# A hybrid diffusion layer: the opening by token halves in written order, matrix-memory pools reused tile by tile, S3 and S4 lows behind the first weight sums

## The chip, the cores and the metric

The kernel runs on one core of one Trainium2 chip, as one program for one launch. The metric is device time in microseconds, the median of several executions. Engines: PE (TensorE, matrix products), DVE (VectorE), ACT (ScalarE), POOL (GpSimd) and SP (SyncE, whose instruction queue issues most transfers).

## The reference

One layer of a diffusion trunk over 640 tokens (512 latent, 128 context), width 1024, feed-forward width 2816, all float32:

```python
def layer(x, mods, l, p, ctx):
    m = [mods[:, j][:, None, :] for j in range(N_MOD)]      # mods = silu(c) @ w_ada + b_ada, 9 x 1024
    g = p['g_norm'][l]
    hh = rmsnorm(x, g[0]) * (1 + m[1]) + m[0]
    x = x + 0.5 * m[2] * swiglu(hh, p['ffn1_w1'][l], p['ffn1_w3'][l], p['ffn1_w2'][l])
    hh = rmsnorm(x, g[1]) * (1 + m[4]) + m[3]
    y, ctx_out = token_mixer(hh, p, l, ctx)      # differential attention || bidirectional mLSTM
    x = x + m[5] * y
    hh = rmsnorm(x, g[2]) * (1 + m[7]) + m[6]
    x = x + 0.5 * m[8] * swiglu(hh, p['ffn2_w1'][l], p['ffn2_w3'][l], p['ffn2_w2'][l])
    return x, ctx_out

def swiglu(h, w1, w3, w2):
    return (jax.nn.silu(h @ w1) * (h @ w3)) @ w2
```

## The kernel before

**Products.** Features lie on partitions, tokens along the free axis, in two halves of 320 (`HALF`). A float32 product is made of three fast ones: each operand is split into a high part (`act(h, raw, Copy)` on ACT) and a low part (`raw - h` on DVE), and `mm3` sums high x high, high x low and low x high. Weights come in granules of 256 output columns, `raw` of 1 MB in a ring of two; of a granule that is used plainly, `wH` and `wL` are the parts.

**Feed-forward up, Strassen-like.** The up products (11 granule pairs of w1 and w3, blocks `b` 0 to 10) run as seven products instead of eight (`Granule`, `HalfStep.products`). Per granule they take weight sums: `parts` makes the small pieces `wB`, `wC` and changes `raw` in place; `sums` then makes the large pair `ww` from it (an ACT pass of 2048 columns and a DVE subtraction, whose instruction is `split_at`). On the token side they take the operands A11, A12, A22 (normed tokens) and S1, S2, S3, S4 (sums of them, high and low), which `operand_sums` makes once, each from two pieces `r`: eight sums `terms` and eight `low` on DVE, eight passes on ACT. Order per granule: A11, S1, S2, A12, S3; the last two, A22 and S4, run inside the next granule. Block 0 is always plain.

**The opening** (`Modulate`): x comes in two half loads; `Stats` makes the sum of squares of each half (ACT squares, DVE adds, `ps_ss` with a matrix of ones sums over partitions), `rstd` its reciprocal root (`rv`, Ln, Exp, and three refining operations of `newton_rsqrt`). For each of the eight feature tiles k, 1 MB of modulation weights is loaded (`raw_a`), `product(k)` (`ps_a`) gives a row, `columns(k)` (`ps_at`) turns it into columns `mod` and `scale`, and `norm` makes the normed tile of both halves, high and low. Block 0's products then run over k, three of its four units at once; the fourth follows. The lows of one of its two weight granules are made on POOL.

**Who sets the order.** A scheduler places instructions on each engine's queue by simulated readiness, within what data and buffers allow. `tc.keep_in_program_order` pins an instruction to the written order (all matmuls are pinned, and the transfers issued by `dma` while `in_order` is set); `tc.issue_after(ins)` holds instructions behind another. A pool with `reuse_waits="tile"` lets a new tile wait for the old tiles that it overlaps; a pool without waits for the whole old pool.

**From attention to matrix memory.** `Fill` is a queue of projection granules whose units are put between the steps of attention; `fill.drain()` runs it empty after the last head, `H.finish()` turns and stores the last head's output (`ps_aT`, `aT`), and `att.close()` gives up attention's pools. Then pools `mp` and `ps3` open, the mask, `csil2` (conditioning, 1 MB) and head 0's `va`, P and C are loaded, and two units of the gate projection `w_gd[1]` and five `prep` steps (`ps_k`, `ps_st`) precede the first cell (`ps_n`). `P` is a row of stabilisers broadcast over partitions, in two loads, plus a mask.

**The second feed-forward** works as the first. Its `operand_sums(…, True)` gives back an instruction (the second low of S2) behind which the next granule's `parts` are held, and a function that makes the lows of S4 later.

Of the kernel before, what the change touches and what calls it, by code (L numbers as in the profile page):

```python
# [31 lines left out]
def tile_trunk(ctx: ExitStack, tc: tile.TileContext, a: dict):  # L32
    nc = tc.nc
    act = nc.scalar.activation
    vec = nc.vector
    pool_e = nc.gpsimd

    def tt(eng, out, in0, in1, op):
        return eng.tensor_tensor(out=out, in0=in0, in1=in1, op=op)  # L39

    def stt(out, in0, scalar, in1, op0, op1):
        return vec.scalar_tensor_tensor(out=out, in0=in0, scalar=scalar, in1=in1, op0=op0, op1=op1)  # L42

    def ts(out, in0, s1, op0, s2=None, op1=None):
        if s2 is None:
            vec.tensor_scalar(out=out, in0=in0, scalar1=s1, scalar2=None, op0=op0)
        else:
            vec.tensor_scalar(out=out, in0=in0, scalar1=s1, scalar2=s2, op0=op0, op1=op1)
# [45 lines left out]
    for hf in range(2):  # L94
        dma(x_all[:, :, hf * HALF : (hf + 1) * HALF], a["x"][:, :, hf * HALF : (hf + 1) * HALF])
    sel = load(cp, [128, 2], a["sel"], name="sel")
    b_ada = load(cp, [128, 72], a["b_ada"], name="b_ada")
    g_norm = load(cp, [128, 3, KT], a["g_norm"], name="g_norm")
# [173 lines left out]
    class Whole(Granule):  # L272


        def split(self, fp=None):
            flat = self.raw.rearrange("p k n -> p (k n)")
            n = 512 * self.nk
            if fp is None:
# [5 lines left out]
            for (c0, c1, h), (_, _, lw) in zip(*t):  # L284
                act(h, flat[:, c0:c1], AF.Copy)
                tt(vec, lw, flat[:, c0:c1], h.bitcast(F32), ALU.subtract)
# [8 lines left out]
    class HalfStep:  # L295
# [29 lines left out]
        def gate_plain(self, f, hf, p):  # L325
            s = self.silu_tile(f, hf)
            act(s, p[0], AF.Silu)
            tt(vec, self.SO[:, self.Q[f, hf]], p[1], s, ALU.mult)

        def operand_sums(self, pair, hold=False):  # L330
# [30 lines left out]
            for f, i, r in (  # L361
                (terms, S1, 0), (terms, S1, 1), (terms, S3, 0), (low, S1, 0), (terms, S2, 0), (low, S1, 1), (terms, S3, 1),
                (terms, S2, 1), (low, S2, 0), (low, S2, 1), (low, S3, 0), (low, S3, 1), (terms, S4, 0), (terms, S4, 1),
            ):
                f(i, r)
                if (f, i) == (low, S2):
                    behind = prev.ins

            def last():
                low(S4, 0)  # L370
                low(S4, 1)

            if hold:
                return behind, last
            last()
            return behind

# [34 lines left out]
        def products(self, work, between, then=(), behind=None, prepared=False):  # L412
# [8 lines left out]
            if not prepared:  # L421
                work[0][0].parts(self.fp)
                work[0][0].sums()
            for i, (gr, A, done, used) in enumerate(work):
# [10 lines left out]
                if not last:  # L435
                    with tc.issue_after(behind if i == 0 and behind is not None else gr.split_at):
                        work[i + 1][0].parts(self.fp)
# [83 lines left out]
        def run_whole(self, x, gate, final, between):  # L521


            work = self.up_work()
# [10 lines left out]
            self.products(work, between, down[:2])  # L535
# [37 lines left out]
        def run(self, x, gate, final, behind=None, after=None):  # L573
# [23 lines left out]
            self.products(work, between, down[:2], behind=behind)  # L597
# [107 lines left out]
    with ExitStack() as ph:  # L705
# [11 lines left out]
        class Modulate:  # L717


            def __init__(self):  # L720
                self.raw, self.row = {}, {}
                self.rs = []
                x = [x_all[:, d, :] for d in range(KT)]
                st = [Stats(x, hf, ntmp) for hf in range(2)]
                for hf in range(2):
                    for d in range(KT):
                        st[hf].add(d)
                    self.rs.append(st[hf].rstd(psum))
                self.load(0)

            def weights(self, w1, w3):

                W = [[wp.tile([128, 2048], F32R, tag="w" + t, name="wH") for t in "HL"] for _ in range(2)]
                raws = [rawp.tile([128, 2048], F32, tag="raw", name="raw") for _ in range(2)]
                for k in range(2):
                    cs = slice(1024 * k, 1024 * k + 1024)
                    for raw, src, (h, lo), eng in zip(raws, (w1, w3), W, (pool_e, vec)):
                        dma(raw[:, cs], src[:, 4 * k : 4 * k + 4])
                        act(h[:, cs], raw[:, cs], AF.Copy)
                        tt(eng, lo[:, cs], raw[:, cs], h[:, cs].bitcast(F32), ALU.subtract)  # L740
                    self.load(k + 1)
                self.load(3)
                return W

            def load(self, k):
                self.raw[k] = load(fp, [128, 2048], a["w_ada_k"][k], tag=("s1", "s2", "s4", "SO")[k % 4], name="raw_a")

            def product(self, k):
# [9 lines left out]
                vec.tensor_copy(self.row[k], ps[:, :256])  # L758
                if k + 4 < KT:
                    self.load(k + 4)  # L760
                if k + 4 == KT - 1:
                    dma(ident, a["ident"])
                    in_order[0] = False

            def columns(self, k):
# [7 lines left out]
                for hf in range(2):  # L773
                    self.norm(hf, k)

            def norm(self, hf, d):

                c0 = hf * HALF
                S = hs.hh(d, hf)
                for s0, s1, j in SEGS[hf]:  # L780
                    xs = x_all[:, d, s0:s1]
                    h, lo = (t[:, s0 - c0 : s1 - c0] for t in S)
                    sh = m_of(0)[:, d, j : j + 1]
# [1240 lines left out]
```

## Time and profile before

| | |
|---|---|
| median of 3 runs | 1869.46 us (1865.64 to 1871.78) |
| profiled execution | 1868.63 us, span 1866.7 us |
| mean granted TensorE clock | 0.99 |
| loads of the first 60 us | 15.38 MB |
| DMA over the span | 299.81 MB, mean 161 GB/s |

How to read the rows. A timeline row has start, duration, engine, line, operation, out<-in, shapes, the number of merged instructions, and in brackets the idle time before it on its engine and what ended it. Line numbers are those of the kernel before; most operations are recorded in a helper (L52 `mm`, L39 `tt`, L42 `stt`, L74 `dma`). A row that begins with `A:B` is a stretch: length, then busy time and count on PE, PEld (weight loads), DVE, ACT and POOL, the mean granted clock, the DMA share and GB/s. Of the page, one row has busy times and shares, another the shares of the chain of waits that ended last.

### The profile page before, as it was taken

The numbers are of one execution on the slowest core, as the hardware profiler recorded it, in microseconds if no ns is written. First come the engines' busy times: TensorE is split into PE (matmuls) and PEld (weight loads), VectorE is DVE, ScalarE is ACT, GpSimd is POOL, SyncE is SP. The second block draws the span as 40 slices with busy tenths as digits, with TensorE's granted clock in tenths as the row PEclk, the third lists the DMA queues.
The fourth block names the chain that finished last, engine by engine and source line by source line (L and its number), as shares of the span: only waits on it lengthen the run. The fifth ranks groups of instructions, "written<-read, shape, count | busy, mean of one in ns | idle before, by whom it ended". The sixth has DMA issues, their size and how long they took to land.

```text
span 1866.7 us, 30740 instructions
## 1 busy us (share of the span) xinstructions
PE 1811.2 (97%) x12658; PEld 1773.0 (95%) x12658; DVE 1303.5 (70%) x2193; ACT 842.6 (45%) x1439; POOL 35.9 (2%) x57
## 2 busy tenths in 40 slices
PE   5899999999999999999999989999999999999999
PEld 4899999999998999999999989999999999999999
DVE  6888886577776675775755537885365878887585
ACT  5644444112454453553544436566234555554232
POOL 1000001110000000000000000000000000000000
PEclk8999999999999999999999999999999999999999
DMA  8344547964324323232222254556533344447872
GB/s 329 119 142 169 192 169 258 373 220 153 104 91 137 116 70 106 89 107 97 98 77 67 94 164 137 187 194 220 186 112 118 110 167 154 175 169 257 328 280 87
DMA packets 127293, 299.81 MB, mean 161 GB/s; under 512 B 9457, under 2 KB 90609, under 8 KB 114353
## 3 DMA queue, kind: packets, MB, share of 16 engines
q1 hardware_dynamic: 117890, 257.49, 39.9%
q0 software_dynamic: 9264, 40.37, 6.0%
q8 instruction: 99, 1.62, 0.4%
q14 instruction: 40, 0.33, 0.1%
HBM read 234.20 MB, written 63.63 MB: 160 GB/s over the span
## 4 chain that ended last, share of the span: by engine, by line
PE 86%; DVE 7%; DMA 4%; ACT 1%; issue 1%; SPq 0%; DVEq 0%; ACTq 0%
PE ps_f L52 40%; PE ps_p L52 22%; PE ps_t L52 12%; PE sc L52 2%; PE ps_o L52 2%; PE ps_n L52 2%; DMA ada<-csil_dram 2%; PE ps_u L52 1%; DVE ww L39 1%; PE ps_wT L55 1%; PE ps_qkT L55 1%; DMA raw<-in_w2b 1%; DMA P<-nm_dram 1%; DMA raw_a<-in_w_ada_c 0%; DVE junk L688 0%
## 5 line engine op out<-in xcount | busy, mean ns | idle before, releaser
L52 PE MATMUL ps_f<-S,ww 128*128 128x320 f32 x1992 | 322.0, 311 | 8.7 <-ACT ww L267 4.2
L52 PEld LDWEIGHTS ps_f<-S,ww 128*128 128x128 f32 x1992 | 300.1, 189 | 11.7 <-DVE ww L39 6.3
L52 PE MATMUL ps_p<-hH,wH 128*128 128x320 f32 x864 | 274.1, 317 | 3.6 <-ACT aT L1337 2.5
L52 PE MATMUL ps_p<-hH,wL 128*128 128x320 f32 x864 | 267.7, 310 | 0.0
L52 PE MATMUL ps_p<-hL,wH 128*128 128x320 f32 x864 | 267.6, 310 | 0.0
L52 PE MATMUL ps_f<-hm,ww 128*128 128x320 f32 x1248 | 198.8, 312 | 2.3 <-DVE ww L39 2.3
L52 PEld LDWEIGHTS ps_f<-hm,ww 128*128 128x128 f32 x1248 | 188.7, 190 | 2.8 <-DVE ww L39 2.6
L52 PE MATMUL ps_t<-wH,hH 128*128 128x256 f32 x640 | 186.4, 291 | 1.0 <-DVE x L42 1.0
L52 PE MATMUL ps_t<-wH,hL 128*128 128x256 f32 x640 | 182.6, 285 | 0.0
L52 PE MATMUL ps_t<-wL,hH 128*128 128x256 f32 x640 | 182.4, 285 | 0.0
L52 PEld LDWEIGHTS ps_p<-hH,wH 128*128 128x128 f32 x864 | 163.0, 189 | 5.0 <-ACT aT L1337 2.7
L39 DVE TENSOR_TENSOR ww<-raw,ww 128x2048 fp32r<-128x2048 f32 (+1 forms) x62 | 138.7, 2237 | 37.0 <-ACT ww L267 21.7
L52 PEld LDWEIGHTS ps_p<-hL,wH 128*128 128x128 f32 x864 | 163.0, 189 | 0.5
L52 PEld LDWEIGHTS ps_p<-hH,wL 128*128 128x128 f32 x864 | 162.8, 188 | 0.0
L52 PE MATMUL ps_f<-hm,wB 128*128 128x320 f32 x1008 | 161.5, 309 | 0.0
L52 PEld LDWEIGHTS ps_f<-hm,wB 128*128 128x128 f32 x1008 | 151.3, 188 | 0.0
L39 DVE TENSOR_TENSOR wL<-raw,wH 128x2048 fp32r<-128x2048 f32 x49 | 112.1, 2288 | 40.2 <-ACT wH L123 40.1
L123 ACT ACTIVATE wH<-raw 128x2048 fp32r<-128x2048 f32 x49 | 93.6, 1911 | 89.6 <-PE ps_p L52 85.1
L39 DVE TENSOR_TENSOR raw<-raw 128x1024 f32<-128x1024 f32 x144 | 124.6, 866 | 1.9
L52 PEld LDWEIGHTS ps_t<-wH,hH 128*128 128x128 f32 x640 | 123.8, 194 | 2.0 <-issue 1.2
L52 PEld LDWEIGHTS ps_t<-wH,hL 128*128 128x128 f32 x640 | 123.9, 194 | 0.5 <-DVE hL L42 0.5
L52 PEld LDWEIGHTS ps_t<-wL,hH 128*128 128x128 f32 x640 | 124.0, 194 | 0.2
(296 smaller groups left out, 3195.3 us busy)
## 6 DMA issues: line engine op xcount, KB each, us to landing
g_dram<-g SPq DMA_DIRECT2D x44, 640.0 KB, 4.3
raw_a<-in_w_ada_c SPq DMA_DIRECT2D x24, 512.0 KB, 4.0
raw<-in_w1b SPq DMA_DIRECT2D x11, 1024.0 KB, 4.8
raw<-in_w3b SPq DMA_DIRECT2D x11, 1024.0 KB, 4.9
raw<-in_w1a SPq DMA_DIRECT2D x10, 1024.0 KB, 4.8
raw<-in_w3a SPq DMA_DIRECT2D x10, 1024.0 KB, 6.1
ada<-in_w_ada_c POOLq DMA_DIRECT2D x18, 512.0 KB, 5.2
hm<-g_dram POOLq DMA_DIRECT2D x7, 1280.0 KB, 9.5
```

The source lines that it names most:

```text
L39: return eng.tensor_tensor(out=out, in0=in0, in1=in1, op=op)
L52: tc.keep_in_program_order(nc.tensor.matmul(*args, **kw))
L55: tc.keep_in_program_order(nc.tensor.transpose(*args, **kw))
L123: act(h, raw, AF.Copy)
```

## The change

**The opening** is rewritten (`Opening`) and by token halves. x comes in four quarters; the order of all loads is written out; the two weight granules of block 0 come in four pieces each, of 0.26 MB. Squares are made over two tiles at a time, half on ACT, half on DVE. Half 0's four units run over k first (`first`, with `step`), and modulation rows and columns, the division by the root, the norm of half 0, the splits of the weights, and half 1's statistics are put between its matmuls; half 1's four units run next (`second`). Between `as_written[0] = True` and `False`, ACT and DVE instructions are pinned to the written order too. POOL does nothing here. Block 1's w1 granule is taken plainly (`Whole`), its parts in tiles that are free at that time, and the Strassen-like granules start with block 1's w3.

**The operand sums.** `operand_sums` now makes S1 and S2, and the terms of S3, and gives back two functions: `third` (the lows of S3), which `products` runs behind the first granule's `split_at`, ahead of the next granule's `parts`; and `fourth` (terms and lows of S4), which both feed-forwards run behind the next granule's `split_at`. In the first feed-forward the column modulation (`csil`, `columns.place`) begins behind `fourth`.

**Matrix memory.** Pools `mp` and `ps3` reuse tile by tile; the granule `w_gd[1]` is queued before the last head ends and kept over `fill.drain(1)`; head 0 is loaded P first, then `va` and C, then `csil2`, in written order.

```diff
+    as_written = [False]
+    def placed(ins):
+        if as_written[0]:
+            tc.keep_in_program_order(ins)
+        return ins
...
-    for hf in range(2):
-        dma(x_all[:, :, hf * HALF : (hf + 1) * HALF], a["x"][:, :, hf * HALF : (hf + 1) * HALF])
+    def load_x(hf, r):
+        dma(x_all[:, 4 * r : 4 * r + 4, hf * HALF : (hf + 1) * HALF], a["x"][:, 4 * r : 4 * r + 4, hf * HALF : (hf + 1) * HALF])
+    for r in range(2):
+        load_x(0, r)
...
             for f, i, r in (
                 (terms, S1, 0), (terms, S1, 1), (terms, S3, 0), (low, S1, 0), (terms, S2, 0), (low, S1, 1), (terms, S3, 1),
-                (terms, S2, 1), (low, S2, 0), (low, S2, 1), (low, S3, 0), (low, S3, 1), (terms, S4, 0), (terms, S4, 1),
+                (terms, S2, 1), (low, S2, 0), (low, S2, 1),
             ):
...
+            return of((low, S3, 0), (low, S3, 1)), of((terms, S4, 0), (terms, S4, 1), (low, S4, 0), (low, S4, 1))
...
+            if ahead is not None:
+                with tc.issue_after(work[0][0].split_at):
+                    behind = ahead()
...
+        def step(ps, k, hf, between=None):
+            h, lo = hs.hh(k, hf)
+            for m, (w, v) in enumerate(((0, h), (1, h), (0, lo))):
+                for (f, i), p in ps.items():
+                    col = 256 * k + 128 * f
+                    mm(p, W[i][w][:, col : col + 128], v, start=k == 0 and m == 0, stop=k == KT - 1 and m == 2)
+                if m == 0 and between is not None:
+                    between()
...
+        load_weights(0)
+        start.load(1)
+        start.load(2)
+        load_x(1, 0)
+        load_weights(1)
+        start.load(3)
+        load_x(1, 1)
+        load_weights(2)
+        psum.order = [4, 5, 6]
+        for r in range(2):
+            start.squares(0, r)
+            start.add_squares(0, r)
+        start.product(0)
+        start.load(4)
+        load_weights(3)
+        start.rstd(0)
+        split_weights(0, "high")
+        start.refine(0)
+        start.columns(0)
+        start.divide(0, 0)
+        start.product(1)
+        split_weights(0, "low")
+        start.norm(0, 0)
+        start.load(5)
...
         for k in range(KT):
+            def ahead(k=k):
+                if k + 1 < KT:
+                    start.columns(k + 1)
+                if k == 5:
+                    start.refine(1)
+                if k >= 6:
+                    start.divide(1, k - 6)
+                if k % 2 and k < 6:
+                    split_weights((k + 1) // 2, "low")
+                elif k % 2 == 0 and k + 2 < KT:
+                    start.divide(0, (k + 2) // 2)
+                if k + 1 < KT:
+                    start.norm(0, k + 1)
+                if k % 2 == 0 and k < 6:
+                    split_weights(k // 2 + 1, "high")
+            step(first, k, 0, ahead)
+            if k + 2 < KT:
+                start.product(k + 2)
+                if k < 2:
+                    start.load(k + 6)
+            if k in (3, 4):
+                start.add_squares(1, k - 3)
+            if k in (1, 2):
+                start.squares(1, k - 1)
+            if k == 4:
+                start.rstd(1)
+            if k >= 6:
+                start.norm(1, k - 6)
...
+        for f, hf in ((0, 1), (1, 1), (0, 0), (1, 0)):
+            p = acc_tile(psum)
             for k in range(KT):
-                hs.plain(ps[i], W[i], 1, 1, k)
...
+                mm3(p, whole.w(0, k, f), whole.w(1, k, f), *hs.hh(k, hf), k == 0, k == KT - 1)
+            gate_first(f, hf, p, None)
+        with tc.issue_after(end.ins), tc.issue_after(at_act.ins):
+            third, fourth = hs.operand_sums(lambda r: x_all[:, 2 * r : 2 * r + 2, :])
...
+            fill.granule(a["w_gd"][1], lambda: feat_units(psum, gate_evac(mp, gd_dram, 1)))
             fill.one()
             fill.one()
-            fill.drain()
+            fill.drain(1)
             H.finish()
...
-    mp = ml.enter_context(tc.tile_pool(name="ml", bufs=1))
-    psum = ml.enter_context(tc.tile_pool(name="ps3", bufs=8, space=PSUM))
+    mp = ml.enter_context(tc.tile_pool(name="ml", bufs=1, reuse_waits="tile"))
+    psum = ml.enter_context(tc.tile_pool(name="ps3", bufs=8, space=PSUM, reuse_waits="tile"))
...
-    mem[0].load()
+    in_order[0] = True
+    mem[0].load(dma)
     mem[0].load_c()
+    csil2 = ada_p.tile([128, 2, D], F32, name="csil")
+    dma(csil2, csil_dram.partition_broadcast(128))
+    in_order[0] = False
+    columns.place(10, csil2, load_columns, 1)
...
-    summed, last_lows = hs.operand_sums(lambda r: x_pairs[r], True)
+    third, fourth = hs.operand_sums(lambda r: x_pairs[r])
```

More of the change, by code (lines that the diff above doesn't have):

```diff
@@ L410, in copy_of, with products @@
             return t
-        def products(self, work, between, then=(), behind=None, prepared=False):
+        def products(self, work, between, then=(), ahead=None, prepared=False):
             n = len(work)
@@ L571, in run_whole, with run @@
                     unit(G[-1], j, f, 1)
[L573 removed]
+        def run(self, x, gate, final, ahead, after):
             def nothing(*args):
@@ L715, in tile_trunk @@
         hs = HalfStep(1, fp, ntmp, psum, a["w1a"], a["w3a"], a["w2a"], FB)
-        class Modulate:
+        class Opening:
             def __init__(self):
[L721 to L743, printed above, removed]
@@ new lines, in tile_trunk @@
+        as_written[0] = True
+        start = Opening()
+        start.load(0)
+        for t, n in ((sel, "sel"), (b_ada, "b_ada"), (g_norm, "g_norm")):
+            dma(t, a[n])
+        load_weights(0)
[11 more added lines that the diff above has]
+        start.product(0)
@@ L842, in tile_trunk @@
+        with tc.issue_after(end.ins), tc.issue_after(at_act.ins):
+            hs.work[0][0].parts(fp)
+            hs.work[0][0].sums()
+        hs.store_g(hs.SO, 0)
         columns = Columns(56)
```

256 lines of the change are left out of this document (147 added, 109 removed).

## The prediction

> **What bounds the kernel now.** I read the page's busy shares and its chain of waits first.
>
> ```profile
> PE 1811.2 (97%) x12658; PEld 1773.0 (95%) x12658; DVE 1303.5 (70%) x2193; ACT 842.6 (45%) x1439; POOL 35.9 (2%) x57
> PE 86%; DVE 7%; DMA 4%; ACT 1%; issue 1%; SPq 0%; DVEq 0%; ACTq 0%
> ```
>
> TensorE is the bound, and 86% of the chain is its work. A change that keeps the matmuls can win only what TensorE loses elsewhere: before its first useful product, in waits, and at half clock after a wait. So I read the timeline for the idle times in its brackets, then the stretches around them for the granted clock (the number after the five engines). First the opening, with the rows of other engines that time its steps:
>
> ```profile
> 8.20 0.47 ACT L177 ACTIVATE nacc<-x 128x320 f32<-128x320 f32 x1 [4.22 <-DMA x<-in_x]
> 12.60 1.43 PE L52 MATMUL ps_ss<-nacc,ones 128*128 128x320 f32 x2 [12.60 <-DVE nacc L39]
> 15.13 0.49 DVE L48 TENSOR_SCALAR rv<-ps_ss 128x320 f32<-128x320 f32 x1
> 16.92 0.49 DVE L42 SCALAR_TENSOR_TENSOR rt<-ry 128x320 f32<-128x320 f32 x1 [0.30 <-ACT ry L160]
> 17.92 2.35 POOL L39 TENSOR_TENSOR wH<-raw,wH 128x1024 fp32r<-128x1024 f32 x1 [17.47 <-ACT wH L739]
> 17.97 2.65 DVE L42 SCALAR_TENSOR_TENSOR ry<-rt,ry 128x320 f32<-128x320 f32 x1
> 19.11 1.58 PE L52 MATMUL ps_a<-raw_a,small 128*32 128x256 f32 x16
> 22.07 0.41 DVE L758 COPY small<-ps_a 128x256 f32<-128x256 f32 x1
> 23.33 0.15 DVE L39 TENSOR_TENSOR mod<-ps_at,b_ada 128x4 f32<-128x4 f32 x1
> 27.60 1.01 PE L52 MATMUL ps_at<-sel,small 128*128 128x2 f32 x4 [3.06 <-DVE small L758]
> 30.41 4.45 PE L52 MATMUL ps_f<-hm,wH 128*128 128x320 f32 x18
> 34.70 0.50 PE L52 MATMUL ps_at<-sel,small 128*128 128x2 f32 x4
> 35.13 1.07 PE L52 MATMUL ps_a<-raw_a,small 128*32 128x256 f32 x16
> 55.98 12.56 PE L52 MATMUL ps_f<-hm,wH 128*128 128x320 f32 x84
> 68.38 1.92 PE L52 MATMUL ps_f<-hm,wB 128*128 128x320 f32 x12
> 84.07 0.56 PE L52 MATMUL ps_f<-S,ww 128*128 128x320 f32 x2 [4.22 <-ACT ww L267]
> 86.40 3.03 PE L52 MATMUL ps_f<-S,ww 128*128 128x320 f32 x10 [1.77 <-DVE ww L39]
> 92.19 1.92 PE L52 MATMUL ps_f<-S,ww 128*128 128x320 f32 x12
> 23.00:34.00 11.00, 7.94 (x52) 5.59 (x52) 9.48 (x21) 5.27 (x11) 2.57 (x1) 0.53 1.02 421
> 85.00:92.00 7.00, 5.60 (x21) 5.60 (x22) 5.60 (x6) 1.91 (x1) 0.00 (x0) 0.51 0.87 307
> ```
>
> The first useful product (`ps_f`) starts at 30.41, and the 11 us that end soon after it ran at a mean clock of 0.53. Block 0 is done at 68.38. Unhindered, a 320-column product takes (68.38 - 55.98) / 84 = 0.148 us. Between 68.38 and 92.19 TensorE did eight groups of twelve; less one group (1.77), the 84 products that a first granule needs were done at 90.42. That is 22.0 us for 12.4 us of work: two waits for the second granule's `ww`, 4.22 and 1.77, and half clock (0.51) behind them. VectorE made the sixteen operations of the S operands ahead of that `ww`.
>
> **Part 1, the opening.** *To the first product.* Work now goes by token halves, so the first product waits for the statistics of half 0 alone. All of half 0 was there at 8.20; in two pieces, the squares of the second piece start then. The 640-wide operations and the other sizes used below:
>
> ```profile
> 61.57 1.55 DVE L39 TENSOR_TENSOR x<-x 128x640 f32<-128x640 f32 x2
> 70.97 0.69 DVE L39 TENSOR_TENSOR wC<-raw,wC 128x512 fp32r<-128x512 f32 x1
> 84.05 2.29 DVE L39 TENSOR_TENSOR ww<-raw,ww 128x2048 fp32r<-128x2048 f32 x1 [1.98 <-ACT ww L267]
> ```
>
> Two VectorE operations of 0.78 bring it to 9.8. The first piece's pair of ones-products (two matmuls with the matrix of ones, 15.13 - 12.60 = 2.5 at this clock) runs beside them, the second pair ends at about 13.0. Then, written in this order: the first modulation product 1.58, its copy 0.41 (it stands ahead of `rv` on VectorE), from `rv` to the first refining step 1.8 as before (16.92 - 15.13), three such steps at 0.49, `mod` and `scale` at 0.15, the division of two tiles 0.78, half an ACT pass of 320 columns 0.47: 13.0 + 1.6 + 0.4 + 1.8 + 1.5 + 0.3 + 0.8 + 0.5 = 19.9, and 0.4 for hand-overs, **20.3 against 30.41, a gain of 10.1**. Part of it is the refining step that took 2.65 beside POOL's 2.35; the change has no POOL work there.
>
> *From there to the end of block 0* was 68.38 - 30.41 = 37.97. The 192 products stay. Past the new starting point lie one more modulation product (1.07), one more `ps_at` (0.50) and half 1's four ones-products (0.6 each at full clock, half of 2.5 / 2): +4.0. The clock: before, TensorE worked from 27.60 and the clock rose at about 34, so 3.5 us of half clock fell on products, a loss of 1.7; now all 6.4 us do, 3.2: +1.5. VectorE and ACT run in written order there. A step with modulation takes TensorE 12 x 0.148 + 1.07 + 0.50 = 3.3; VectorE has in step 1 two weight lows (1.38), two squares (1.56), `mod`/`scale`, a 320-wide low and a copy (1.2): 4.1; in step 5 three refining steps (1.5), two lows (1.4) and 1.2: again 4.1. So I allow +1.7 for these two; in the other steps VectorE has 2 to 3. Sum +7.2, **block 0 ends at about 65.5, 2.9 earlier**.
>
> *The first granule.* Its w1 is now multiplied plainly: 96 products, 14.2, instead of 84 in 22.0. They need no S operand and hide VectorE's work on those: ten operations at 0.78 for S1, S2 and their lows, the next weights' sums with their ACT pass, gating. S1 and `ww` are due at 65.5 + 14.2 + 1.8 = 81.5. VectorE's second-half work needs only what is loaded by then, so it can start on the S operands near 61: ten at 0.78, two gates and one store's low (2.5), parts of the weights (five operations, 4.5 from the 0.69 row and twice that for the double width), the wait for ACT's pass 2.0, `ww` 2.29, together 19.1: ready at 80. If that cover is gone it costs what the rival below says. The next granule's parts, the S3 lows (1.6) and its `ww` then come out within 0.5 of their due time: +0.5. Term: 14.2 + 0.5 - 22.0 = -7.3. **Opening: -10.2**; between -14 (no VectorE delay, earlier clock, no wait) and -2 (a start 3 later, both delays doubled, the rival's wait).
>
> On the clock, this trace has 6.4 us from steady work to full clock. The Trainium skill (TensorE: Matmul & The Clock Gate, Part 1) has the gate open after one busy window of about 3.4 us of a free-running counter. This trace took longer; by the page's figure the sum would be 1.5 us lower.
>
> The change moves the column modulation's 1 MB load, its ACT pass and its POOL loads behind the first granule's sums; its first user is a granule later, some 10 us away, so I cost it at nothing; without that cover, the brackets of 1.77 to 4.22 us above are the size of one such wait.
>
> **Part 2, from attention to matrix memory.**
>
> ```profile
> 1101.00 0.41 PE L52 MATMUL ps_p<-hH,wH 128*128 128x320 f32 x1 [2.47 <-ACT aT L1337]
> 1103.26 0.32 SPq L1553 DMA_DIRECT2D csil<-csil_dram  x1
> 1104.69 3.87 SPq L1579 DMA_DIRECT2D P<-nm_dram  x2
> 1114.18 0.83 DVE L39 TENSOR_TENSOR P<-P,mask 128x640 f32<-128x640 f32 x1 [10.55 <-DMA P<-nm_dram]
> 1117.46 1.20 PE L52 MATMUL ps_n<-va,P 128*128 128x258 f32 x2 [4.29 <-DVE P L39]
> 1102.00:1106.00 4.00, 4.00 (x19) 4.00 (x18) 0.27 (x5) 0.00 (x0) 0.00 (x0) 0.57 0.83 208
> 1116.00:1123.00 7.00, 5.54 (x14) 4.44 (x15) 4.56 (x12) 4.65 (x17) 0.00 (x0) 0.52 0.92 296
> ```
>
> Four losses: the first product waits 2.47 for the last ACT copy, because the new PSUM pool waits for the whole old one; half clock follows, 4 x 0.43 = 1.7; `ps_n` waits 4.29 for P; half clock again, (1123 - 1117.46) x 0.48 = 2.7. Together 11.2. With waits by tile the first product takes a bank whose evacuation is older: I take 2.2 and 1.6 of the first two. P is now the first load of SP's sequence there, ahead of `va`, C and the 1 MB of `csil`, which was ahead of it. Issued even as late as 1103.3, two issues of 1.9 and a transfer of about as much land it at about 1109; mask, ten ACT passes and the product with `ps_st` need some 3 more us, so `ps_n` can start where `ps_st` ends, 4.3 earlier. I take 3.6 and 2.0 of these two, leaving the rest to `va` and C. Who is queued behind P on SP are `va`, C, `csil`, and stores of `stage`; the column tile that reads `csil` comes several cells later. **-9.4**; between -11.2 and 0, 0 if both pools' tiles still wait for the last reader.
>
> **Part 3, the second feed-forward's S operands.**
>
> ```profile
> 1483.57 2.29 DVE L39 TENSOR_TENSOR ww<-raw,ww 128x2048 fp32r<-128x2048 f32 x1 [4.00 <-ACT ww L267]
> 1485.91 1.73 PE L52 MATMUL ps_f<-S,ww 128*128 128x320 f32 x10 [1.64 <-DVE ww L39]
> ```
>
> A loss of 1.64, no fall of the clock. Two S4 terms (1.55) leave VectorE's queue ahead of this `ww`, but VectorE idles 4.00 for ACT's pass, which an earlier `raw` only partly moves: I take -1.0, between -1.6 and +1.6 (the moved operations are then late for S4, whose product is three groups, 5.3 us, further).
>
> **Sum.** -10.2 - 9.4 - 1.0 = -20.6. The profiled execution took 1868.63 (span 1866.7), so 1848.0; it stands 0.8 under the median of the three runs (1869.46), so **1848.8**. With the better ends, 1841.
>
> **The rivals.** *P still late.* If P's tile overlaps one that attention reads last, SP waits as before, behind `mask`. Against: `csil` is behind it now. For: the profile doesn't show which tile overlaps. Only 3.8 of 9.4 remain: 1854.4. *VectorE late.* If the S operands start only when block 0 ends, 65.5, the 19.1 us end at 84.6, 3.1 late; the next granule's parts, `ww` and S3 lows add 1.5, and two half-clock stretches like the one at 85 to 92 cost 1.7 each: +8.0, 1856.8. For it: before, VectorE was the releaser of exactly these waits.
>
> *Slower: the opening becomes bound by its loads.* The first half now needs all eight modulation loads in lock step, 13.1 MB by the shapes in the code, in smaller pieces.
>
> ```profile
> GB/s 0 23 224 375 374 365 356 401 396 407 437 421 388 423 429 431 410 421 415 421 437 421 399 415 410 426 421 177 20 0 0 11 0 0 0 0 0 0 0 0
> HBM read 234.20 MB, written 63.63 MB: 160 GB/s over the span
> ```
>
> At the rates of this row (1.5 us a number) the last of them is there at about 36, and its product is due only after step 5, near 43; that speaks against. At the span's mean of 160 GB/s it would land at 2.5 + 82 = 84, and 5 us of last steps, then 28.4 for the second half and the granule, end at 117.5, 27 later than 90.4; with parts 2 and 3 gained, 1886. It turns the change into a loss beyond a landing at 67.5 (33.4 before 90.4 + 10.4), which is 200 GB/s. A rule of the Trainium skill speaks for it (DMA: Bandwidth & Descriptors, Bandwidth): batch to 1 MiB or more for 75% of peak, while 64 KB reach 32%. The trace's 0.5 MB pieces, queued behind one another, ran at the rate of the row all the same.
>
> *The change doesn't do what it says*: pools still wait whole, and the order written down stalls as often as it saves; within 0.3%.
>
> **How the numbers follow.** Forecast 0.62, with 1842 to 1853 of its own; P late 0.16; VectorE late 0.12, both of them (1862) 0.03; loads 0.04; no change 0.03. 0.3% is about what a measurement of this kernel can tell from no change, 5.6 us. Faster 0.93, same 0.03, slower 0.04. The range takes in the forecast and each of the two middle rivals: 1841 to 1860.
>
> **What would show it.** The first `ps_f` near 20; block 0 ending near 65; no bracket over 1 us on `ps_f<-S,ww` up to 100; `ps_n` following `ps_st` with no bracket, and a clock of 1.0 from 1080 to 1110 of the new time; the row of 1485.91 about 20 earlier with a shorter bracket. I am wrong if the first steps show brackets on `ps_at` or `ps_a` for DMA, if `ww` shows up again at 80, or if P's bracket stays.

## The result and the profile after

| | before | after |
|---|---|---|
| median, us (5 runs each) | 1867.77 (1865.64 to 1871.78) | 1856.69 (1856.58 to 1860.09) |
| profiled execution, us (span) | 1868.63 (1866.7) | 1856.65 (1854.9) |

The ratio is 0.9943, 95% interval 0.9927 to 0.9959: faster by 11 us, where 20.6 were forecast. First the same two lines of the page of the changed kernel: busy time by engine, and the chain that ended last.

```profile
PE 1810.4 (98%) x12678; PEld 1771.0 (95%) x12678; DVE 1299.3 (70%) x2181; ACT 834.7 (45%) x1419; POOL 30.9 (2%) x55
PE 83%; DVE 7%; DMA 6%; ACT 2%; issue 1%; SPq 0%; DVEq 0%; ACTq 0%
```

TensorE's busy time is 0.8 us less and its idle time 11.0 us less (55.5 to 44.5): nearly all of the 11.8 us of span are idle time that went. To see where, take one event and compare its start in both traces. The timeline of the changed kernel, TensorE's rows (start, length, what it does, idle time before it and its releaser):

```profile
7.42 4.06 PE L59 MATMUL ps_ss<-sq,ones 128*128 128x320 f32 x8 [7.42 <-DVE sq L46]
11.40 1.07 PE L59 MATMUL ps_a<-raw_a,small 128*32 128x256 f32 x16
...
15.04 1.07 PE L59 MATMUL ps_a<-raw_a,small 128*32 128x256 f32 x16 [1.42 <-DMA raw_a<-in_w_ada_k]
17.69 1.44 PE L59 MATMUL ps_f<-hm,wH 128*128 128x320 f32 x4 [1.58 <-ACT hm L43]
...
32.31 0.61 PE L59 MATMUL ps_at<-sel,small 128*128 128x2 f32 x4 [0.50 <-DVE small L790]
...
46.06 0.61 PE L59 MATMUL ps_at<-sel,small 128*128 128x2 f32 x4 [1.12 <-DVE small L790]
...
63.80 0.46 PE L59 MATMUL ps_f<-hm,wgA 128*128 128x320 f32 x2
...
77.88 1.92 PE L59 MATMUL ps_f<-hm,wB 128*128 128x320 f32 x12
...
89.93 0.56 PE L59 MATMUL ps_f<-S,ww 128*128 128x320 f32 x2 [1.30 <-ACT ww L43]
92.25 2.71 PE L59 MATMUL ps_f<-S,ww 128*128 128x320 f32 x10 [1.76 <-DVE ww L46]
...
104.16 1.92 PE L59 MATMUL ps_f<-hm,wB 128*128 128x320 f32 x12
```

and, of the kernel before, the row that answers to the last of these (A11 of the same granule) and four later joints (only the starts are used; a row at the edge of a view shows only the part inside it): the first query product, the last head's `ps_wT`, the first product after matrix memory, the second feed-forward's first product; then the same four of the changed kernel.

```profile
111.55 1.63 PE L52 MATMUL ps_f<-hm,wB 128*128 128x320 f32 x10
...
488.36 0.36 PE L52 MATMUL ps_t<-wH,hH 128*128 128x256 f32 x1 [0.99 <-DVE x L42]
1026.13 0.33 PE L55 MATMUL ps_wT<-ident,p 128*128 128x128 f32 x1 [0.70 <-DVE p L42]
1242.75 0.41 PE L52 MATMUL ps_p<-hH,wH 128*128 128x320 f32 x1 [0.41 <-ACT num L1622]
1443.18 0.46 PE L52 MATMUL ps_f<-hm,wH 128*128 128x320 f32 x2
```

```profile
479.16 0.36 PE L59 MATMUL ps_t<-wH,hH 128*128 128x256 f32 x1 [0.98 <-DVE x L49]
1018.15 0.33 PE L62 MATMUL ps_wT<-ident,p 128*128 128x128 f32 x1 [0.70 <-DVE p L49]
1230.75 0.41 PE L59 MATMUL ps_p<-hH,wH 128*128 128x320 f32 x1 [0.44 <-ACT num L43]
1431.09 0.46 PE L59 MATMUL ps_f<-hm,wH 128*128 128x320 f32 x2
```

The lead grows and shrinks like this: 12.7 at the first product (30.41 to 17.69), 4.6 at the end of block 0, 12.5 when the first granule's work is done (90.42 to 77.88), **7.4** two granules later, at the fourth one's first product (111.55 to 104.16), 9.2 at 479 (a bracket on `ww` near 350 is 1.06 instead of 2.34), 8.0 at 1018, **12.0** at 1231, 12.1 at the second feed-forward, 11.8 at the end. Two places need a reading: the fall from 12.5 to 7.4, and why the transition at 1100 gave 4.0.

*The fall.* VectorE and ScalarE between 77 and 92 of the changed kernel:

```profile
77.51 2.29 DVE L46 TENSOR_TENSOR ww<-raw,ww 128x2048 fp32r<-128x2048 f32 x1 [0.98 <-ACT ww L43]
79.72 1.55 DVE L46 TENSOR_TENSOR S<-x,S 128x640 fp32r<-128x640 f32 x2
...
82.93 1.49 DVE L46 TENSOR_TENSOR g<-SO,g 128x1280 fp32r<-128x1280 f32 x1
...
85.87 1.41 DVE L46 TENSOR_TENSOR raw<-raw 128x512 f32<-128x512 f32 x2
...
89.91 2.29 DVE L46 TENSOR_TENSOR ww<-raw,ww 128x2048 fp32r<-128x2048 f32 x1 [0.78 <-ACT ww L43]
```

```profile
86.17 0.63 ACT L43 ACTIVATE wC<-raw 128x512 fp32r<-128x512 f32 x1 [2.35 <-DMA raw<-in_w3a]
86.71 1.04 ACT L43 ACTIVATE wB<-raw 128x1024 fp32r<-128x1024 f32 x1
...
87.97 1.90 ACT L43 ACTIVATE ww<-raw 128x2048 fp32r<-128x2048 f32 x1
```

The first Strassen-like granule's `ww` is ready in time (no bracket at 79.64). The second one's has on VectorE's queue ahead of it the S3 lows that the change put there (1.55), the parts, block 0's gated values (1.49) and the weight changes, to 87.3. ScalarE's pass takes from 87.97 to 89.9, VectorE's to 92.2, and TensorE stops for both. ScalarE could have begun at 87.3, but made two pieces of the following granule first, whose load had just landed: up to 0.7 of the 1.30 is its order, and the rest stands behind VectorE's queue.

*The transition.* SP's, VectorE's, ScalarE's and TensorE's rows of the changed kernel:

```profile
1094.56 0.42 SPq L81 DMA_DIRECT2D mask<-in_mask  x1
1095.03 0.99 SPq L81 DMA_DIRECT2D P<-nm_dram  x2
```

```profile
1100.34 0.83 DVE L46 TENSOR_TENSOR P<-P,mask 128x640 f32<-128x640 f32 x1 [6.14 <-DMA P<-nm_dram]
1102.27 0.82 DVE L46 TENSOR_TENSOR P<-P,mask 128x640 f32<-128x640 f32 x1 [1.10 <-DMA P<-nm_dram]
```

```profile
1101.20 1.57 ACT L43 ACTIVATE P<-P,cols 128x128 f32<-128x128 f32 x5 [6.65 <-DVE P L46]
1102.67 0.41 ACT L43 ACTIVATE stage<-ps_p 128x320 f32<-128x320 f32 x1
```

```profile
1103.14 1.22 PE L59 MATMUL ps_st<-mqT,mkT 128*128 128x128 f32 x4 [3.33 <-ACT stage L43]
...
1105.44 1.07 PE L59 MATMUL ps_n<-va,P 128*128 128x258 f32 x2
```

The pools do what the change says: no bracket after `ps_aT`. P is ahead of `csil`, and `ps_n` doesn't wait for it. But on ScalarE five passes over P stand ahead of a `stage` copy that needs only a product finished long before, and that copy frees the PSUM bank that `ps_st` needs. The wait for P came back as a wait for ScalarE.

The clock, in windows (columns: stretch, length, busy time of PE, PEld, DVE, ACT and POOL, granted clock, DMA share, GB/s):

```profile
17.58:24.41 6.83, 6.72 (x34) 5.12 (x35) 3.22 (x8) 3.06 (x6) 0.00 (x0) 0.50 1.05 393
92.67:96.09 3.42, 3.42 (x15) 3.42 (x14) 3.42 (x6) 1.47 (x2) 0.00 (x0) 0.50 0.80 287
1103.02:1106.43 3.41, 3.29 (x13) 3.10 (x14) 2.01 (x6) 3.37 (x12) 0.00 (x0) 0.50 1.05 417
```

The last two rows stand behind the two stops: half clock for 3.4 us costs about 1.7 more at each.

### The profile page after: what moved, and what is told of

Read it like the earlier page. It is cut to its first block, busy times and chain, and to the rows that moved or that the text cites. A ratio compares the mean times of both kernels' runs of the same rounds, so it can differ in the third digit from the quotient of the medians.

```text
span 1854.9 us, 30739 instructions
## 1 busy us (share of the span) xinstructions
PE 1810.4 (98%) x12678; PEld 1771.0 (95%) x12678; DVE 1299.3 (70%) x2181; ACT 834.7 (45%) x1419; POOL 30.9 (2%) x55
## 4 chain that ended last, share of the span: by engine, by line
PE 83%; DVE 7%; DMA 6%; ACT 2%; issue 1%; SPq 0%; DVEq 0%; ACTq 0%
PE ps_f L59 39%; PE ps_p L59 21%; PE ps_t L59 12%; PE sc L59 2%; PE ps_o L59 2%; DMA ada<-csil_dram 1%; DVE ww L46 1%; PE ps_n L59 1%; PE ps_qkT L62 1%; PE ps_wT L62 1%; DMA raw_a<-in_w_ada_c 1%; DMA raw<-in_w2b 1%; PE ps_u L59 1%; DMA a_raw<-aT_dram 1%; DMA hm<-g_dram 1%
## 5 line engine op out<-in xcount | busy, mean ns | idle before, releaser
L59 PE MATMUL ps_f<-S,ww 128*128 128x320 f32 x1956 | 315.3, 310 | 5.8 <-DVE ww L46 4.0
L59 PEld LDWEIGHTS ps_f<-S,ww 128*128 128x128 f32 x1956 | 294.0, 188 | 8.5 <-DVE ww L46 6.9
L59 PE MATMUL ps_f<-hm,ww 128*128 128x320 f32 x1236 | 195.0, 310 | 1.5 <-DVE ww L46 1.1
L43 ACT ACTIVATE ww<-raw 128x2048 fp32r<-128x2048 f32 (+1 forms) x61 | 114.1, 1870 | 152.1 <-PE ps_f L59 104.0
L59 PE MATMUL ps_f<-hm,wB 128*128 128x320 f32 x984 | 157.7, 309 | 0.0
L43 ACT ACTIVATE wH<-raw 128x2048 fp32r<-128x2048 f32 (+1 forms) x57 | 98.1, 1728 | 88.1 <-PE ps_p L59 83.5
```

The costliest lines, as they stand in the source:

```text
L43: return placed(nc.scalar.activation(*args, **kw))
L59: tc.keep_in_program_order(nc.tensor.matmul(*args, **kw))
```

## Experiments

All times are medians in us, with the ratio to the kernel before on the same chip (its medians there were 1866.9 to 1867.4) and its 95% interval. The edits are shortened to the lines that matter; a comment stands for what is left out.

**The parts alone.** The opening alone (with the second feed-forward's operands in the order before), the transition alone, the second feed-forward's order alone:

```diff
 e1: -    third, fourth = hs.operand_sums(...)          # second feed-forward
 e1: +    third, fourth = hs.operand_sums(..., True)    # S3 lows and S4 terms ahead, as before
 e2:  only the pools with reuse_waits="tile", P ahead of va, csil behind both, drain(1)
 e3:  only the second feed-forward's S3 and S4 lows behind the first granules' sums
```

> The opening alone, with the second feed-forward's operand order and the pools of matrix memory as before. Theory: the three parts act at three places and add up; the opening is worth what the two traces show between the start and the end of the first feed-forward, 9.2 us (488.36 against 479.16 for the first ps_t), so about 0.4 to 0.5% faster, and the waits for P (4.29) and for aT (2.47) are in its trace as they were. Rival: what the later parts lose (four idle times over 0.8 us after 1000 us that the kernel before lacks) comes from the opening's shift of the scheduler's clock; then this kernel alone shows such new idle times after 1000 us too, and gains less than 8.

> The pools of matrix memory alone (tile by tile, P first, w_gd[1] queued early, csil2 later). Theory: the PSUM half of it is gained (no bracket of 2.47 on ps_p, no half clock at that place: 4.0), and P is still late, so TensorE stops for it at ps_st instead of ps_n, for about 3.3 and half clock: in all 3 to 5 us faster than before. Rival (the prediction's 9.4): P is late in the changed kernel only because other loads collide there; alone it gains 8 to 10.

> The second feed-forward's operand order alone (S3 lows and S4 behind the weight sums). Theory: the wait of 1.64 for ww at the second granule goes, and one of about the same size for the third granule's ww takes its place, since the S4 operations and the store of block 0 now stand in front of that; net within 1 us of before. Rival (the prediction): 1.0 us faster, no bracket on ps_f at the third granule.

Measured: 1861.80, ratio 0.9971 (0.9962 to 0.9981); 1862.44, 0.9970 (0.9959 to 0.9982); 1868.06, 1.0001 (0.9988 to 1.0013). The parts add up: 0.29 + 0.30 - 0.01 is 0.58%, the whole is 0.57%. The opening alone shows the two `ww` waits (1.18 at 91.83, 1.77 at 94.16), the transition alone the 3.25 on `stage`. The opening gained 5.3 us where 9.2 were expected: its trace is 7.0 ahead at the first query product (488.36 to 481.40), and the stop for P behind it grew from 4.29 to 5.72. Of its rival only the small gain came true: after 1000 us no stop over 0.8 stands that the kernel before lacks. Of the third, TensorE's row at the third granule:

```profile
1497.98 1.73 PE L52 MATMUL ps_f<-S,ww 128*128 128x320 f32 x10 [1.32 <-DVE ww L39]
```

The bracket of 1.64 at the second granule is gone, and 1.32 stands at the next. The wait moved on by a granule.

**More cover for P.** Four projection units instead of two ahead of the memory stage:

```diff
-    fill.one()
-    fill.one()
+    for _ in range(4):
+        fill.one()
```

> The changed kernel, with four units of w_gd[1] ahead of the prep steps instead of two; the two more are taken from the fill of the cells. Theory: TensorE stops at ps_st for P's transfer, which lands some 6 us after its issue; 7 us more of matmuls in front cover the wait: the bracket of 3.33 goes and so does the stretch of half clock behind it (1.7): 4 to 5 us faster than the changed kernel, 0.8 to 0.9% faster than before. Rival: the stop is ACT's order alone (the stage copy stands behind the P passes whenever they come); then the bracket moves behind the two units and stays as long, and the time is the same within 1 us or worse, as the cells lack two fill units.

Measured: 1857.92, 0.9952 (0.9938 to 0.9966); cover alone gains nothing over the changed kernel. ScalarE's row and TensorE's:

```profile
1112.29 0.44 ACT L43 ACTIVATE stage<-ps_p 128x320 f32<-128x320 f32 x1 [3.06 <-DMA gd_dram<-stage]
```

```profile
1112.78 0.69 PE L62 MATMUL ps_k<-ident,mkT 128*128 128x128 f32 x2 [3.74 <-ACT stage L43]
```

The `stage` ring has two tiles. The store of the first was issued at 1103.29, behind P, `va`, C and `csil` on SP, and landed 8.9 us later. A stop of the same size, with the same engine at its head, has another cause.

**P from another queue, P in longer runs.** First P and the mask issued by POOL; then P's tile as [128, 2, 5, 128], so that each partition receives 2560 bytes in a run instead of 512.

```diff
-    mem[0].load(dma)
+    mem[0].load(dma, nc.gpsimd.dma_start)     # e5: P (and mask) from POOL's queue
```
```diff
-    self.P = mp.tile([128, 5, 2, 128], ...)
+    self.P = mp.tile([128, 2, 5, 128], ...)   # e9
```

> The changed kernel, with head 0's P and the mask fetched from POOL's queue, so that they don't stand behind the store of aT, which SP issues at 1093.0, nor behind raw_a. Theory: P is late because it is issued late (1095.0); on a queue that waits for nothing but its tile, whose old users are done by the last scores, it lands several us earlier, the bracket of 3.33 on ps_st and the half clock behind it (1.7) go: 4 to 5 us faster than the changed kernel (about 1852). Rival: the transfer itself is slow (6.7 us from issue to landing for 0.66 MB); from POOL's queue it lands no more than 2 us earlier, and the time stays within 1.5 us.

> The changed kernel, with P laid out as two rows of 640 per partition, so that each load writes one run of 2560 bytes per partition instead of five of 512. Theory (slow transfer): the loads land in 3 to 4 us instead of 6.7, TensorE's wait at ps_st shrinks from 3.33 to about 1 and the half clock with it: 2 to 4 us faster than the changed kernel. Rival (late issue): the transfer is as long as before, as it shares the queue with 0.5 MB of raw_a and the mask; no change within 1 us.

Measured: 1864.02, 0.9988 (0.9978 to 0.9998), and 1859.41, 0.9957 (0.9943 to 0.9971): 7.3 and 2.7 slower than the changed kernel. In e5 one of P's two mask additions ran at 1097.2; then ScalarE stood on `va`, and TensorE after it:

```profile
1104.46 0.91 ACT L43 ACTIVATE wv<-va,cols 128x258 f32<-128x258 f32 x2 [6.82 <-DMA va<-v_dram]
```

```profile
1105.74 1.22 PE L59 MATMUL ps_st<-mqT,mkT 128*128 128x128 f32 x4 [2.85 <-ACT stage L43]
1114.10 1.20 PE L59 MATMUL ps_n<-va,P 128*128 128x258 f32 x2 [5.85 <-issue]
```

`ps_n` at 1114.10 stood for P after all. VectorE's waits, with total, number and longest:

```profile
DVE P L46 <- DMA P<-nm_dram: 12.0, 2, 11.2
```

The two are for the loads that SP issued at 1100.36 and 1102.53, head 1's, which landed 8.8 and 8.3 us later. Head 0's second mask addition, the last of the four, came behind them at 1111.6, and P's first product with `ps_st` at 1113.57, ending 0.1 us ahead of `ps_n`. The early transfer only chose who waits. In e9 P's median landing is 7.3 us against 6.7: short runs were not what made it late.

**ScalarE in VectorE's place in the opening.** Half 1's modulated x made by ScalarE, in all feature tiles (e6) or in every second (e7):

```diff
-    if hf:
+    if hf and d % 2:                          # e7; in e6 never
         ts(xs, xs, sc, ALU.mult, sh, ALU.add)
```

> The changed kernel, with the scaled and shifted x of half 1 made on ACT in one pass, as for half 0, instead of on VectorE. It takes eight pairs of 0.63, 5 us, off VectorE before 60 us and puts some 7 us on ACT. Theory: VectorE, busy without a gap from 54 to 75 us and the releaser of the waits of 1.30 and 1.76 for ww near 90, is the bound of this stretch; with 5 us less it is through some 3 us earlier, the wait for ww there falls under 1 in all and no half clock follows: 3 to 5 us faster than the changed kernel. Rival: ACT's order binds (its passes for ww wait behind pieces of the next granule whose load has just come); then the wait stays, and ACT with 7 us more delays half 1: same or up to 3 us slower.

> As the last, but only for the even feature tiles: 2.5 us off VectorE, 3.5 us on ACT. Theory (VectorE binds): about half of its gain, 1.5 to 3 us faster than the changed kernel. Rival (ACT's order binds): no gain, within 1 us.

Measured: 1860.27, 0.9966 (0.9953 to 0.9979), and 1861.34, 0.9970 (0.9955 to 0.9984): 3.6 and 4.7 slower than the changed kernel. ScalarE becomes the pace (in e6 TensorE waits 2.15 for it at 67), and the waits for `ww` stay (0.76 and 1.77 at 94 in e6; 0.99, 1.70 and 1.38 at 94, 109 and 123 in e7). The rival's sign is there: ahead of the stop at 109 ScalarE makes two pieces of the following granule, each after 1.2 us of waiting for TensorE, and starts its `ww` pass at 104.28, though VectorE's last change of `raw` had ended at 102.8. Freeing VectorE before 60 us by loading ScalarE is no gain; these two runs don't decide about VectorE's queue.

**VectorE's low parts to POOL.** S3's lows and block 0's gated low:

```diff
-    tt(vec, g[:, 1], SO[:, c0:c1], ...)
+    tt(nc.gpsimd, g[:, 1], SO[:, c0:c1], ...)     # block 0; S3's two lows likewise
```

> The changed kernel with two low parts taken off VectorE and given to GpSimd: S3's two low parts in the first FFN (1.55 us of VectorE ahead of the second Strassen granule's weights) and the low part of block 0's gated values (1.49 us). Theory (VectorE's queue is late there: 3.04 us of it stand ahead of the weights whose two waits are 1.30 and 1.76 us): both waits go, and the half clock behind them; ps_t comes 3 to 5 us earlier and the time is 1852 to 1854. Rival (the queue is late by more than one granule, so that the wait moves on, as from granule to granule before): stops of 1 us or more come at the third or fourth granule, and no more than 1.5 us are gained. Second rival (GpSimd's passes slow VectorE's own, which work at the same time): VectorE's passes of 2048 columns take over 2.4 us instead of 2.29, and nothing is gained.

Measured: 1859.58, 0.9959 (0.9946 to 0.9972). The second rival. POOL's and VectorE's rows:

```profile
72.45 8.26 POOL L46 TENSOR_TENSOR S<-x,S 128x640 fp32r<-128x640 f32 x2 [72.00 <-ACT S L43]
81.53 4.14 POOL L46 TENSOR_TENSOR g<-SO,g 128x1280 fp32r<-128x1280 f32 x1 [0.83 <-ACT g L43]
```

```profile
79.77 3.09 DVE L46 TENSOR_TENSOR ww<-raw,ww 128x2048 fp32r<-128x2048 f32 x1 [0.50 <-ACT ww L43]
82.78 3.98 DVE L46 TENSOR_TENSOR wB<-raw,wB 128x1024 fp32r<-128x1024 f32 x1
```

VectorE's pass of 1024 columns took 3.98 beside POOL instead of 1.22, that of 2048 3.09 instead of 2.29; the 3.04 us that were taken off came back as 3.6 in these two passes. The first rival's sign is there too, stops of 1.70 at 110 and 1.38 at 124; ahead of the first of them ScalarE again made two pieces of the following granule, and started its `ww` pass 1.9 us after VectorE's last change of `raw`.

**A second plain granule.** Block 1's w3 is taken plainly too: 12 more products, but VectorE has less to do for it and 14 us more ahead of the first Strassen granule.

```diff
+    _, _, gate_next, _ = hs.work.pop(0)
+    whole2 = Whole(4, hs.up[1].fetch)             # then load, split, 96 products, gate_next
-    hs.run_whole(..., lambda i, at: modulation(i + 1, at), third)
+    hs.run_whole(..., lambda i, at: modulation(i + 2, at), third)
```

> The changed kernel with block 1's second weights (w3) taken as a plain granule too: 96 products in place of 84, so 12 more of 147 ns or 1.8 us of TensorE, but VectorE saves 1.9 us of parts and 2.6 us of weight changes for that granule and has 14.1 us more before the first Strassen granule's weights are due. Theory (in the opening VectorE's queue is late, by about the two waits of 1.30 and 1.76 us and the half clock behind them): these stops and the half clock go, none of over 1 us stands before 150 us, and net of the 1.8 us the time is 2 to 3.5 us below the changed kernel's, 1853 to 1855. Rival (the first Strassen granules' chain of weight changes, ScalarE's copy and low part is too long in itself, however early it may begin): the stops come again at the second or third Strassen granule, now some 14 us later, and the time is 1.5 to 2 us above the changed kernel's, 1858 to 1859.

Measured: **1854.35**, 0.9929 (0.9915 to 0.9943), 2.3 below the changed kernel's median. The two intervals overlap, so the times alone don't show a gain; the stretch itself does. Windows of this kernel:

```profile
64.00:80.00 16.00, 16.00 (x111) 16.00 (x110) 14.70 (x21) 11.34 (x18) 0.00 (x0) 1.00 0.36 132
80.00:110.00 30.00, 30.00 (x207) 30.00 (x206) 24.11 (x28) 13.32 (x17) 1.22 (x2) 1.00 0.57 197
```

TensorE is busy all 46 us at full clock; the only bracket on `ww` up to 200 is 0.15, at 155. From the end of block 0 to the fourth granule's first product it is 36.96 us (66.12 to 103.08) against 40.36 (63.80 to 104.16), with 12 products more. The traced execution (1858.03, the slowest of its six) lost this again elsewhere: it starts at 19.46, and stops for 2.97 at 351 and 4.77 at 1104. The wait didn't move on, so that `ww` was late by a bounded amount, and cover and work taken off VectorE together end it. Which of the two does more, and how much is ScalarE's order, was not tried.

**The transition's order.** For head 0, all `ps_k` first, then all `ps_st`, then a third projection unit with a stage tile of its own; on ScalarE the passes over P behind the last `mktok` copy, `wv` behind these, head 1's mask, passes and gate behind the first cells:

```diff
-    for i in range(5):
-        mem[0].prep(i)
+    for i in range(5): mem[0].keys(i)             # ps_k, mktok
+    for i in range(5): mem[0].scores(i)           # ps_st
+    with tc.issue_after(mem[0].copied.ins):
+        for i in range(5): mem[0].weigh(i)        # exponentials of P, product with ps_st
+    with tc.issue_after(mem[0].copied.ins):
+        fill.one()
```

> The changed kernel with only the start of the memory stage reordered for its first head: all five key transposes with their ScalarE copies first, then all five score products, then one more unit of the 96-product projections with a stage tile of its own; ScalarE's exponentials of P held behind the last key copy, the va scalings behind the exponentials, head 1's mask sums, exponentials and gate behind the first cells. Theory (in the changed kernel the stop of 3.33 us at ps_st, and the half clock of 3.4 us behind it, come from ScalarE's order: a stage copy that needs nothing stands behind five passes over P, which lands 6.7 us after its issue): the stop and the half clock go, no stop over 1 us stands between the last ps_aT and the first ps_n, and the time is 3 to 5 us below the changed kernel's, 1852 to 1854. Rival (the transfers set the pace, whatever stands in which order): a stop of 3 us or more comes back at the first cells, on va or on P, and the time stays within 1 us of the changed kernel's.

Measured: **1853.25**, 0.9922 (0.9907 to 0.9937), 3.4 below the changed kernel, with overlapping intervals again. ScalarE, TensorE and the window:

```profile
1100.63 0.44 ACT L43 ACTIVATE stage<-ps_p 128x320 f32<-128x320 f32 x1 [3.08 <-PE ps_p L59]
1100.96 1.49 ACT L43 ACTIVATE mktok<-ps_k 128x256 f32<-128x256 f32 x5
1105.83 0.40 ACT L43 ACTIVATE P<-P,cols 128x128 f32<-128x128 f32 x1 [3.38 <-DVE P L46]
```

```profile
1107.81 0.67 PE L59 MATMUL ps_n<-va,P 128*128 128x258 f32 x2 [0.37 <-DMA va<-v_dram]
```

```profile
1095.00:1112.00 17.00, 16.24 (x108) 14.94 (x107) 7.25 (x16) 8.37 (x25) 0.00 (x0) 1.00 0.88 286
```

P is no earlier (ScalarE still idles 3.38 for it), yet TensorE has 0.37 of a stop and the clock stays at 1.00. From the first query product to the second feed-forward it is 947.9 us (481.78 to 1429.69) against 951.9; from the last head's `ps_wT` to the first product after matrix memory it is 208.2 (1021.15 to 1229.36) against 212.6, and 211.2 to 214.1 in e4, e6, e7 and e9. It was the order, the cover and the stage tile together: cover alone (e4) ended at another copy on ScalarE. The order alone was not tried, so how the gain divides stays open.

**Both together.**

> The changed kernel with both edits together: block 1's second weights as a plain granule, and the reordered start of the memory stage. They touch stages 1000 us apart. Theory (the two losses are separate): the gains add, 2.3 and 3.4 us by the medians of the two runs, so about 1851 and a ratio to the kernel before of 0.991. Rival (what is gained early is lost at later joints, such as the stop at 350 us, which has ranged from 1.4 to 3.3 us between runs): 1853 to 1855.

Measured: **1849.97** (1848.54 to 1853.71), 0.9911 (0.9897 to 0.9926): faster than both kernels, 6.7 below the changed one where the two gains make 5.7, and here the intervals don't overlap.

```profile
64.00:110.00 46.00, 46.00 (x316) 46.00 (x315) 38.00 (x43) 25.76 (x34) 1.21 (x2) 1.00 0.53 190
```

From the end of block 0 to the fourth granule it is 36.96 us again (63.11 to 100.07); in the transition the longest stop is 0.17, at full clock from 1080 to 1112. The losses were separate. What is left of the places discussed is a bracket of 2.86 at 348 on a `ww`, which ranges from 1.06 to 2.97 over the runs, and the 1.32 at the second feed-forward's third granule.

## Why the prediction was right or wrong

The sign was right, and the time lay in the range; the forecast of 1848.8 was 7.9 too low. The two large terms had the right sign and were too large, the opening with 7.4 of 10.2, the transition with 4.0 of 9.4. Some of what came true is luck: the traced start of 17.69 is the earliest of all the runs with this opening, and by its own run (e1) the opening is worth 5.3. That the time is also the figure of the rival "VectorE late" (1856.8) is chance, for more than half of what is missing was missing in the transition. By its steps:

- *The first product*: 20.3 forecast, 17.69 measured, in spite of 1.42 on `raw_a` and 1.58 on ScalarE. The ones-products ended at 11.5 instead of 13.0, and the modulation product took 1.07 instead of 1.58. This start ranges from 17.7 to 19.5 over the kernels with the same opening.
- *To the end of block 0*: 45.2 forecast, 46.1 measured; of the 1.7 allowed for steps 1 and 5 (counted from 0, as in the code), TensorE shows 0.50 in step 3 and 1.12 in step 6, both for the copy of `small`; the second stands behind step 5's refining operations and weight lows on VectorE. The end was 4.6 earlier, not 2.9.
- *The first granule*: 14.2 forecast, 14.08 measured, without a wait: "ready at 80" was met, `ww` came out at 79.8.
- *The step that failed in the opening* is the last term: the next granule's `ww` "within 0.5 of its due time". It was late by 1.30 and 1.76, with 1.7 of half clock behind: 4.8. The rival "VectorE late" had the right mechanism at the wrong granule. I had counted VectorE's work up to the first granule; for the next I named its parts, the S3 lows and `ww`, and gave a size to the lows alone, where the whole queue from 79.7 counts, the gated values' 1.49 and the weight changes included, and up to 0.7 of ScalarE's order. e12 agrees: with 46 us of TensorE's work and less of VectorE's, no wait is left. Opening at 104: 7.4 of 10.2.
- *The transition*: 9.4 forecast, 4.0 measured (216.62 us of stage to 212.60; TensorE's idle time in it fell by 2.1, its busy time, by the clock, by 1.9). The 2.47 after `ps_aT` and its half clock went, as forecast. The step that failed is "`ps_n` can start where `ps_st` ends": P did arrive earlier, but the path to `ps_n` leads through ScalarE's queue, where P's passes stood ahead of a bank's evacuation. The outcome is that of the rival "P still late" (3.8); its cause, SP waiting for P's tile, is not what happened. P was issued at 1095.03, 2 us behind the last store.
- *The second feed-forward*: 1.0 forecast, nothing gained by e3 (1.0001, 0.9988 to 1.0013). That the bracket would go was right; it came back a granule later, which the term didn't ask.
- *Loads-bound opening*: TensorE shows one wait of 1.42 on `raw_a`, nothing later. The rule against small pieces (the Trainium skill, DMA: Bandwidth & Descriptors, Bandwidth) had no effect to show here: between 17.58 and 24.41 the queue moved 393 GB/s.
- *The clock gate*: I wrote that 6.4 us passed to full clock against the Trainium skill's one window of 3.4 us. In the changed kernel the half-clock stretches last 3.42, 3.41 and 6.83, one or two times 3.41, and the first stretch of e12 lasts 10.2, three times, with TensorE idle for 22% of it. These lengths agree with the free-running window of the Trainium skill (TensorE: Matmul & The Clock Gate, Part 1). That one busy window is enough they don't show: TensorE was busy for 6.72 of the 6.83. The first stretch differs from run to run (3.4 to 10.2 us), and what sets it stays open.
- *Two sums*: the five operations on the weights' parts come to 4.8 by the widths and the 0.69 row, not 4.5 (the trace has 4.5); the better ends of the three terms, 26.8 together, give 1842.7, not 1841. Neither moves the forecast.

## What to carry to other kernels

When a wait is removed on one granule of a pipeline, count the engine's queue up to the next granule's due time too: an engine that is late by a fixed amount shows its wait one granule later. Here more cover together with less work for that engine ended it; work moved to an engine that slowed it did not. An engine's order counts as much as an arrival: an instruction that waits for a transfer holds every ready copy behind it, and through a PSUM bank or a two-tile ring the matmuls, so put what frees banks ahead of what waits. Bring forward one of several competing loads only after asking which of the others will then be last.

## What the runs showed of the hardware

- Subtractions on POOL and VectorE at the same time slowed each other in e11: POOL took 4.1 us for 640 columns, where the kernel before had 2.35 for 1024, and VectorE 3.98 for 1024 columns instead of 1.22, though its passes between 72.9 and 77.1 took their usual 0.82 and 0.69. The Trainium skill names a cause (SBUF — State Buffer, Who interferes with whom: the shared port pair is an exclusive lock); the trace agrees in kind.
- A store of 160 KB, issued behind loads on the same queue, took 8.9 us to land in e4, against 1.8 for the stores of the same size just before the loads (median of two).
- P's landing did not become shorter with longer runs: 6.7 us at 512 bytes, 7.3 at 2560 (two loads each).
